# Attention outputs with queries on partitions, elementwise work off GpSimd, and a shorter reciprocal root

## The chip, the cores and the metric

One core of a Trainium2 chip runs the whole program. The metric is the device time of one execution in microseconds (us), as the median over runs. A profile shows one execution: its engines are TensorE (PE; PEld is its weight load), VectorE (DVE), ScalarE (ACT), GpSimd (POOL) and SyncE (SP, which issues the transfers).

## The reference

A first block (linear recurrence, long convolutions, 16 experts) is followed by two attention layers with MLPs, all in float32 on 512 positions of width 1024. The change lies in the attention layers and in the last norm. Each layer has four kinds of attention with four heads of 64 value columns: latent attention (M), differential attention (D), a window with sinks (S) and a neighbourhood with a bias table (N). Three of the four outputs get a norm over 256 columns, the differential one a norm per head:

```python
    for l in range(DEPTH_2):
        h = rms_norm(x, norm1_g[l])
        proj = h @ w_in[l]
        ...
        mix = jnp.concatenate([rms_norm(y_a, out_g_mla[l]), y_b,
                               rms_norm(y_c, out_g_swa[l]), rms_norm(y_d, out_g_na[l])], axis=-1)
        x = x + mix @ w_out[l]
        h = rms_norm(x, norm2_g[l])
        x = x + jnp.square(jax.nn.relu(h @ w_up[l])) @ w_down[l]
    return rms_norm(x, final_norm_g)
```

with, in every attention, `p = softmax(q k * scale)`, `o = p v`; in D `w = p0 - lam * p1`, `o = w v`, and `rms_norm(o, subln_g) * (1 - lambda_init)` for each head.

## The kernel before, in words

Activations lie with features on partitions and the 512 positions along the row, as 8 tiles `x` of 128 x 512. Large products are made of three passes on rounded halves (`mm3`, lines 161 to 165): each operand is split into a rounded part and the remainder (`split`, lines 147 to 158, the rounded part on ACT, the remainder on DVE or POOL). Weights stream through `WStream.get` (line 222) in the same manner.

A layer's attention (lines 398 to 842) is a list of steps written out by hand (`CFG["order0"]`, `CFG["order1"]`, lines 21 and 22; interpreted from line 792): projections (`b`, `c`, `d`, `v`, `u`), operands of the scores (`m`, `e`, `s`, `q`, `k`), pairs of heads in halves of two query blocks (`M0a`, `D1b`), norms (`nM`, `n0`, `n1`, `nS`, `nN`), the split of finished outputs (`x`) and the output projection in two parts (`W`, `V`). When the program is built, a planner places every instruction on its engine's queue by this order and by its own estimate of durations, and instructions then run in that order on each engine.

For one block of 128 queries and one head, `softmax_tile` (line 542) makes the scores in PSUM, DVE takes the row extreme, ACT the exponential with the row sum; M, S and N then scale the 128 x n tile by the reciprocal of the sum on DVE (`normed`, line 607). In D the second tile is folded into the first with a factor that holds both sums (lines 705 to 707), and the first sum is left to the norm. `transposed` (line 592) turns P by TensorE with up to four 128 x 128 transposes, and ACT (for M every other time DVE) copies it out. `pv` (line 610) then multiplies: V's 64 columns of a head are stationary, 128 queries stream, and the two heads of a pair write PSUM partitions 0 to 63 and 64 to 127 of one tile `o`, features on partitions:

```python
        for a, j in enumerate(js):
            for s in range(2):
                nc.tensor.matmul(o[s * 64:(s + 1) * 64, q], v[:, j, vc[s]:vc[s] + 64], pts[s][:, a],
                                 start=a == 0, stop=a == len(js) - 1)
```

`ysq` (line 631) copies `o` and squares it on ACT. `out_norm` (line 638) adds two squares on DVE, sums columns by matmuls with ones (line 190), takes the reciprocal root on DVE (`rsqrt`, lines 168 to 180, eleven small instructions), spreads the result over partitions by four diagonal tiles and a matmul (`bcast_cols`, line 204), and scales (line 647). `diff_norm` (line 711) does the same per head with two column sums (line 715) and two broadcasts into 64 partitions each (lines 726 to 730). `split_held` (line 627) splits the results on ACT and POOL.

On POOL in a layer are: the remainders of `hilo_rows` (line 539), of the S keys, the N keys (line 533), the small weights (line 493) and the outputs (line 625); and the two multiplies of `roped` (lines 449 and 450, for the b and c heads only the first). In the first layer also the remainders of the first three weight tiles (line 456). At the end of the program `last_half` (line 324) sums eight squares on DVE, and one of four final scalings is on POOL (line 347).

Of the kernel before, what the change touches and what calls it, by code (L numbers as in the profile page):

```python
# [6 lines left out]
F32 = mybir.dt.float32  # L7
F32R = mybir.dt.float32r
# [10 lines left out]
CFG = dict(acc=2, o=1, S=3, tp=2, qk=9, H=9, y=5, z=7, P=5, PT=2, sb=4, R=4, raw=3, sp=2, rp=3, rb=1,  # L19
           lm=1, le=0, ls=0, lq=0, lk=0, fM=2, fD=100, fS=100, fN=100, rB=1, rC=1, wi=1, wo=1, xs=0, ul=0,  # L20
# [147 lines left out]
def rsqrt(c, v, n):  # L168

    nc = c.nc  # L170
    t = c.small.tile([128, 8], I32, name="rq_t", tag="rq_t")[:, :n]
# [32 lines left out]
def bcast_cols(c, cols, psp, tag, out, scale=1.0):  # L204
# [8 lines left out]
    nc.scalar.activation(out, ps, AF.Copy, scale=scale)  # L213
    return ps
# [30 lines left out]
def body_t2(c, A, x, out, gain=None):  # L245
# [5 lines left out]
    with ExitStack() as ctx:  # L251
        ws = c.ws = WStream(c, ctx.enter_context(pool("w", 3, side="right")), CFG["raw"], CFG["sp"])
        pers = ctx.enter_context(pool("t2"))
        c.blk = pers.tile([128, 2], F32, name="blk")
        nc.vector.memset(c.blk, 0.0)
        nc.vector.memset(c.blk[0:64, 0:1], 1.0)
        nc.vector.memset(c.blk[64:128, 1:2], 1.0)
# [11 lines left out]
        def sumsq(tiles):  # L269
            s = None  # L270
            for t in tiles:
                q = hp.tile([128, T], F32, name="sq", tag="sq", bufs=3)
                nc.scalar.activation(q, t, AF.Square)
                if s is None:
                    s = q
                else:
                    nc.vector.tensor_tensor(s, s, q, op=OP.add)
            return s
# [45 lines left out]
        def last_half(l, ff, s, cols, mp):  # L324

            sq, xg = None, []
            for m in range(KD):
# [7 lines left out]
                if m == 0:  # L335
                    sq = q
                else:
                    nc.vector.tensor_tensor(sq, sq, q, op=OP.add)
# [4 lines left out]
            rb = mp.tile([128, T], F32, name="rbf", tag="rbf", bufs=2)[:, :256]  # L343
            ps = bcast_cols(c, rs, ps_t, "tp", rb)
# [53 lines left out]
def attention(c, A, l, h, rsb, cols, lam_init, ap, hp, ws, ps_acc, ps_o, ps_s, ps_t, x, rx, gain):  # L398
# [57 lines left out]
    e = "pool" if rx is not None else "dve"  # L456
    cq0 = compact(proj(0, acc=spsum, lo_eng=e, late=late), rsb)
    cq1 = compact(proj(1, 96, acc=spsum, lo_eng=e, late=late), rsb)
    ckv = compact(proj(2, acc=spsum, lo_eng=e, late=late), rsb)
    kpe = roped(cq1, 0, slice(64, 96))  # L460
# [44 lines left out]
    roped(qn[2], 0)  # L505
# [36 lines left out]
    def softmax_tile(passes, i, js, bias=None, op=OP.min, init=None, sm=None):  # L542
# [26 lines left out]
        if init is not None:  # L569
            es = c.small.tile([128, 1], F32, name="es", tag="es")  # L570
            nc.scalar.activation(es, init, AF.Exp, bias=mn, scale=sgn)
            nc.vector.tensor_tensor(sm, sm, es, op=OP.add)
# [34 lines left out]
    def normed(p, rc):  # L607
        nc.vector.tensor_scalar(p, p, rc, None, op0=OP.mult)
# [9 lines left out]
    def emit_mixed(z):  # L618
        held.append(z)

    def split_mixed(z):
        hi = hp.tile([128, T], F32R, name="hh", tag="hh")
        lo = hp.tile([128, T], F32R, name="hl", tag="hl")
        split(c, z, hi, lo, lo_eng=ENG[CFG["xs"]])
        mixed.append((hi, lo))
# [12 lines left out]
    def out_norm(yqs, g0, perm=False):  # L638
        (y0, q0), (y1, q1) = yqs
        nc.vector.tensor_tensor(q0, q0, q1, op=OP.add)  # L640
        r = rs_cols(c, q0, 256, ps_acc, "acc")
        rb = ap.tile([128, T], F32, name="rb", tag="rb", bufs=CFG["rb"])
        bcast_cols(c, r, ps_acc, "acc", rb)
        for i, y in enumerate((y0, y1)):
            z = ap.tile([128, T], F32, name="z", tag="z", bufs=CFG["z"])
            v = (lambda a: a.rearrange("p (w r) -> p w r", r=8)) if perm else (lambda a: a)
            nc.vector.scalar_tensor_tensor(wr(z) if perm else z, v(y), cols[:, g0 + i:g0 + i + 1], v(rb),
                                           op0=OP.mult, op1=OP.mult)
            emit_mixed(z)
# [18 lines left out]
    def mla_pair(pair, ops, o, tiles):  # L668
        for i in tiles:
            pts = []  # L670
            for s in range(2):
                p, sm = softmax_tile(ops[s], i, full)
                normed(p, reciprocal(sm))
                pts.append(transposed(p, full, "M"))
# [20 lines left out]
    def diff_pair(pair, ops, o, tiles):  # L695

        if pair not in sums:
            sums[pair] = ap.tile([128, 4, 2], F32, name="sms", tag="sms", bufs=2)
        sms = sums[pair]
# [11 lines left out]
    def diff_norm(yq, sms):  # L711
        y, q = yq
        ps = acc()
        for i in range(4):
            nc.tensor.matmul(ps[:, 2 * i:2 * i + 2], q[:, i * 128:(i + 1) * 128], c.blk, start=True, stop=True)
        v = c.small.tile([128, 8], F32, name="dv", tag="dv", bufs=2)
        u = c.small.tile([128, 8], F32, name="du", tag="du", bufs=2)
        rc = sms.rearrange("p i s -> p (i s)")
        nc.vector.reciprocal(rc, rc)
        nc.vector.tensor_tensor(u, rc, rc, op=OP.mult)  # L720
        nc.vector.tensor_tensor(v, u, ps[:, :8], op=OP.mult)
        nc.vector.tensor_scalar(v, v, 1.0 / 64, EPS, op0=OP.mult, op1=OP.add)
        r = rsqrt(c, v, 8)
        nc.vector.tensor_tensor(r, r, rc, op=OP.mult)
        rb = acc()
        for s in range(2):
            d = c.diag.tile([128, 4, 128], F32, name="diag", tag="diag")
            for i in range(4):
                nc.vector.tensor_scalar(d[:, i], c.ident, r[:, 2 * i + s:2 * i + s + 1], 1.0 - lam_init, op0=OP.mult, op1=OP.mult)
            nc.tensor.matmul(rb[s * 64:(s + 1) * 64], c.ones[:, :64], d.rearrange("p a b -> p (a b)"), start=True, stop=True)  # L730
        z = ap.tile([128, T], F32, name="z", tag="z", bufs=CFG["z"])
        nc.vector.scalar_tensor_tensor(z, y, cols[:, 25:26], rb, op0=OP.mult, op1=OP.mult)
        emit_mixed(z)
# [12 lines left out]

    def swa_pair(g, qs, o, tiles):
        for i in tiles:
# [3 lines left out]
            for n in range(2):  # L752
                p, sm = softmax_tile([(qs[n], kops[n][0]), (qs[n], kops[n][1])], i, js,
                                     bias=band[:, b0:b0 + 128 * len(js)], init=nsk[:, 2 * n + g:2 * n + g + 1])
                normed(p, reciprocal(sm))
                pts.append(transposed(p, js, "S"))
            pv(o, i, pts, vb, [256, 320], js)

# [9 lines left out]
    def na_pair(pair, ops, o, tiles):  # L768
        qs, ks = ops
        for i in tiles:  # L770
# [4 lines left out]
            for s in range(2):  # L775
                tab = ap.tile([128, 384], F32, name="nab", tag="sb", bufs=CFG["sb"])[:, :n]
                nc.sync.dma_start(tab, A["nab"][l, pair * 2 + s][:, at:at + n])
                p, sm = softmax_tile([(qs[s], ks[s][0]), (qs[s], ks[s][1])], i, js, bias=tab, op=OP.max)
                normed(p, reciprocal(sm))
# [12 lines left out]
    for step in CFG["order%d" % l].split():  # L792
# [35 lines left out]
        elif step in ("n0", "n1"):  # L828
            diff_norm(ys["D", n], sums[n])
        elif step == "nM":  # L830
            out_norm((ys["M", 0], ys["M", 1]), 19)
        elif step == "nS":
            out_norm((ys["S", 0], ys["S", 1]), 21)
        elif step == "nN":
            out_norm((ys["N", 0], ys["N", 1]), 23, perm=True)
# [982 lines left out]
```

## Time and profile before

| | |
|---|---|
| median of 3 runs | 2930.9 us (2928.51 to 2931.96) |
| the profiled execution's own time | 2928.38 us |
| its span in the profile | 2926.6 us |
| PE busy | 2782.9 us, 95% |
| DVE busy | 1541.2 us, 53% |
| ACT busy | 923.7 us, 32% |
| POOL busy | 177.5 us, 6% |

The busy share is a mean over stages with different limits. Attention of the first of the two layers lies at about 1575 to 1890 us of the span, of the second at 2253 to 2560, each followed by its MLP; the last MLP ends with the final norm and the stores. Matmuls are pipelined, so the busy time of a group of them holds their tails; the time that one costs is read from one start to the next.

### The profile page before, as it was taken

Reading aid. Unit: us, or ns where it says so; the run is one execution under the profiler, and the core shown is the slowest. Engines: PE = TensorE matmul, PEld = TensorE weight load, DVE = VectorE, ACT = ScalarE, POOL = GpSimd, SP = SyncE. Lnnn points to the kernel's source line nnn. Section 1 sums busy time; section 2 is a strip of 40 time slices with the busy share of each in tenths; the row PEclk is TensorE's granted clock in tenths of the full one; section 3 lists DMA queues with packets and bytes.
Section 4 is the critical chain, followed back from the end, with each engine's and each line's share of the span. In section 5 each row is a group of like instructions: output and inputs, shape, how many; then the busy total and the mean of one; then the engine's idle time right before and its main releaser. Section 6 shows DMA issues by size and latency. Waiting matters only on the chain.

```text
span 2926.6 us, 35016 instructions
## 1 busy us (share of the span) xinstructions
PE 2782.9 (95%) x13300; PEld 1844.3 (63%) x13300; DVE 1541.2 (53%) x3121; ACT 923.7 (32%) x1553; POOL 177.5 (6%) x150
## 2 busy tenths in 40 slices
PE   8999999999999999998898899999999999999998
PEld 6878888763333333333334676788887776788887
DVE  7878899642212212222114889654445789644436
ACT  5656332220000000000002367433323377433324
POOL 0000000000000000000000233000000333000000
PEclk9999999999999999999999999999999999999999
DMA  4443333589999999999996233223223332222223
GB/s 161 155 158 138 117 109 123 165 333 413 420 421 421 420 420 421 421 421 421 421 421 266 79 83 80 81 94 101 94 94 121 94 85 76 86 94 94 95 98 132
DMA packets 136352, 617.89 MB, mean 211 GB/s; under 512 B 17423, under 2 KB 31575, under 8 KB 84600
## 3 DMA queue, kind: packets, MB, share of 16 engines
q1 hardware_dynamic: 136184, 615.65, 55.6%
q8 instruction: 105, 1.72, 0.2%
q14 instruction: 63, 0.52, 0.1%
HBM read 582.03 MB, written 16.78 MB: 205 GB/s over the span
## 4 chain that ended last, share of the span: by engine, by line
PE 78%; DMA 8%; DVE 8%; issue 3%; ACT 1%; POOL 1%; SPq 0%; DVEq 0%; ACTq 0%; POOLq 0%
PE acc L165 11%; PE acc L164 11%; PE acc L163 11%; PE gps L1665 11%; DMA ew<-experts 8%; PE dps L1690 5%; PE S L163 4%; PE S L164 4%; PE S L165 4%; PE fps L1197 2%; PE o L615 2%; PE acc L1717 2%; PE acc L1618 2%; PE S L549 2%; PE tp L598 1%
## 5 line engine op out<-in xcount | busy, mean ns | idle before, releaser
L152 ACT CAST wh<-wr 128x1024 fp32r<-128x1024 f32 (+3 forms) x294 | 291.7, 993 | 819.5 <-PE acc L164 510.6
L1665 PE MATMUL gps<-ew,xe 128*64 128x512 f32 x2048 | 489.1, 597 | 9.1 <-DMA ew<-experts 8.9
L155 DVE TENSOR_TENSOR wl<-wr,wh 128x1024 fp32r<-128x1024 f32 (+3 forms) x291 | 335.8, 1156 | 68.7 <-ACT wh L152 67.8
L1665 PEld LDWEIGHTS gps<-ew,xe 128*64 128x64 f32 x2048 | 151.0, 137 | 286.0 <-issue 253.4
L163 PE MATMUL acc<-hh,wh 128*128 128x512 f32 x768 | 312.1, 406 | 0.1
L165 PE MATMUL acc<-hh,wl 128*128 128x512 f32 x768 | 307.2, 400 | 3.0 <-DVE wl L155 2.8
L164 PE MATMUL acc<-hl,wh 128*128 128x512 f32 x768 | 308.4, 402 | 0.0
L1690 PE MATMUL dps<-ew,hT 128*64 128x512 f32 x992 | 225.1, 600 | 15.2 <-DMA ew<-experts 8.8
L164 PE MATMUL acc<-fl,wh 128*128 128x512 f32 (+1 forms) x576 | 213.5, 371 | 0.0
L165 PE MATMUL acc<-fh,wl 128*128 128x512 f32 (+1 forms) x576 | 213.4, 371 | 0.0
L163 PE MATMUL acc<-fh,wh 128*128 128x512 f32 (+1 forms) x576 | 213.2, 370 | 0.0
L165 PE MATMUL S<-hh,wl 128*128 128x512 f32 x512 | 199.9, 391 | 0.0
L164 PE MATMUL S<-hl,wh 128*128 128x512 f32 x512 | 199.0, 389 | 0.0
L163 PE MATMUL S<-hh,wh 128*128 128x512 f32 x512 | 198.9, 389 | 0.0
L1673 DVE TENSOR_TENSOR g<-g,gps 128x512 f32<-128x512 f32 x32 | 21.9, 685 | 331.0 <-PE gps L1665 322.3
L1690 PEld LDWEIGHTS dps<-ew,hT 128*64 128x64 f32 x992 | 74.8, 138 | 156.4 <-issue 128.4
L165 PEld LDWEIGHTS acc<-hh,wl 128*128 128x128 f32 x768 | 145.8, 190 | 37.3 <-DVE wl L155 6.3
L163 PEld LDWEIGHTS acc<-hh,wh 128*128 128x128 f32 x768 | 146.3, 191 | 35.7 <-issue 6.1
L164 PEld LDWEIGHTS acc<-hl,wh 128*128 128x128 f32 x768 | 146.1, 190 | 31.8 <-issue 4.2
L395 DVE TENSOR_TENSOR x<-acc,x 128x512 f32<-128x512 f32 x56 | 38.8, 692 | 184.2 <-PE acc L165 184.2
L1672 ACT ACTIVATE g<-gps 128x512 f32<-128x512 f32 x32 | 19.2, 599 | 366.3 <-PE gps L1665 353.8
L379 DVE SCALAR_TENSOR_TENSOR r<-S,rsb 128x512 f32<-128x512 f32 x64 | 44.1, 692 | 162.3 <-PE S L165 158.6
(400 smaller groups left out, 4503.5 us busy)
## 6 DMA issues: line engine op xcount, KB each, us to landing
ew<-experts SPq DMA_DIRECT2D x384, 1024.0 KB, 19.8
wr<-w_down SPq DMA_DIRECT2D x72, 512.0 KB, 3.3
wr<-w_up SPq DMA_DIRECT2D x64, 512.0 KB, 3.3
wr<-w_in SPq DMA_DIRECT2D x56, 512.0 KB, 4.5
wr<-in_w SPq DMA_DIRECT2D x38, 512.0 KB, 3.3
R<-qkc SPq DMA_DIRECT2D x72, 128.0 KB, 2.3
filters_dram<-K SPq DMA_DIRECT2D x8, 1024.0 KB, 3.9
K<-filters_dram SPq DMA_DIRECT2D x8, 1024.0 KB, 6.7
```

Of the source, the lines that this page charges most:

```text
L152: nc.scalar.copy(hi, src)
L155: (nc.vector if lo_eng == "dve" else nc.gpsimd).tensor_tensor(lo, src, hi.bitcast(F32), op=OP.subtract)
L163: nc.tensor.matmul(ps, W[0], X[0], start=start, stop=False)
L164: nc.tensor.matmul(ps, W[0], X[1], start=False, stop=False)
L165: nc.tensor.matmul(ps, W[1], X[0], start=False, stop=stop)
L549: nc.tensor.matmul(ps, q[:, qs], k[:, ks], start=a == 0, stop=a == len(passes) - 1)
L615: nc.tensor.matmul(o[s * 64:(s + 1) * 64, q], v[:, j, vc[s]:vc[s] + 64], pts[s][:, a], start=a == 0, stop=a == len(js) - 1)
L1197: nc.tensor.matmul(ps[:, half * Q:(half + 1) * Q], dft[:, s], v[:, r], start=True, stop=True)
L1618: nc.tensor.matmul(ps[h * 64:(h + 1) * 64], sel[:, i], rows[i][h], start=i == 0, stop=i == 3)
L1665: nc.tensor.matmul(ps[h * 64:(h + 1) * 64], xes[e][:, kt], W[:, k, h * T:(h + 1) * T], start=kt == 0, stop=kt == 7)
L1690: nc.tensor.matmul(outs[e][col * 64:(col + 1) * 64], hT[:, j, p * 64:(p + 1) * 64], W[:, p, h * T:(h + 1) * T], start=cc == 0 and j == 0 a ...
L1717: nc.tensor.matmul(ps, Y[f // 4][j][:, (f % 4) * 128:(f % 4 + 1) * 128], st[f // 4], start=j == 0, stop=j == n - 1)
```

## The change

1. `pv` swaps its operands: P is stationary (128 x 128), a head's 64 V columns stream, and the output has queries on partitions, with the two heads side by side along the row. All key blocks of the first head come before those of the second.
2. M, S and N no longer scale P. The row sums of a pair go into a small tile (128 x 4 blocks x 2 heads), as in D before. `ysq` adds a row sum of the squares per block and head on DVE. The norms work on these small tiles: reciprocals, squares, a sum over heads for M, S and N, `rsqrt`, and one multiply of the 128 x 512 output by the factors (`scaled_rows`). Column sums, diagonals and broadcasts of the output norms are gone.
3. `split_held` first transposes each finished output (four 128 x 128 transposes into PSUM), and the split applies the gain, the rounded part on ACT and the remainder on DVE.
4. All remainders and the multiplies of `roped` go to DVE; so does the last scaling at the end, straight from PSUM.
5. `rsqrt` has nine instructions instead of eleven.
6. `sumsq` and `last_half` hand the last square to the column-sum matmuls as a second tile instead of adding it on DVE.

```diff
-           lm=1, le=0, ls=0, lq=0, lk=0, ..., rB=1, rC=1, wi=1, wo=1, xs=0, ul=0,
+           lm=1, le=1, ls=1, lq=1, lk=1, ..., rB=2, rC=2, wi=1, wo=1, ul=1,
...
 def rsqrt(c, v, n):
-    nc.vector.tensor_scalar(t, v.bitcast(I32), 1, None, op0=OP.logical_shift_right)
-    nc.vector.tensor_scalar(y.bitcast(I32), t, -1.0, 1597463007.0, op0=OP.mult, op1=OP.add)
-    for _ in range(3):
-        nc.vector.tensor_tensor(u, y, y, op=OP.mult)
-        nc.vector.scalar_tensor_tensor(u, u, -0.5, v, op0=OP.mult, op1=OP.mult)
-        nc.vector.scalar_tensor_tensor(y, u, 1.5, y, op0=OP.add, op1=OP.mult)
+    nc.vector.tensor_scalar(y.bitcast(I32), v.bitcast(I32), -0.5, 1597463007.0, op0=OP.mult, op1=OP.add)
...
+    nc.vector.tensor_scalar(w, u, 1.5, 2.5, op0=OP.mult, op1=OP.add)
+    nc.vector.tensor_tensor(w, w, u, op=OP.mult)
+    nc.vector.scalar_tensor_tensor(y, w, 1.875, y, op0=OP.add, op1=OP.mult)
...
-                if j == 0:
-                    nc.gpsimd.tensor_tensor(t, t, rb[:, None, :].to_broadcast([128, 2, 256]), op=OP.mult)
-                else:
-                    nc.vector.tensor_tensor(t, t, ps[:, None, :].to_broadcast([128, 2, 256]), op=OP.mult)
+                nc.vector.tensor_tensor(t, t, ps[:, None, :].to_broadcast([128, 2, 256]), op=OP.mult)
...
     def pv(o, i, pts, v, vc, js):
-        q = slice(i * 128, (i + 1) * 128)
-        for a, j in enumerate(js):
-            for s in range(2):
-                nc.tensor.matmul(o[s * 64:(s + 1) * 64, q], v[:, j, vc[s]:vc[s] + 64], pts[s][:, a],
+        for s in range(2):
+            for a, j in enumerate(js):
+                nc.tensor.matmul(o[:, i * 128 + s * 64:i * 128 + (s + 1) * 64], pts[s][:, a], v[:, j, vc[s]:vc[s] + 64],
                                  start=a == 0, stop=a == len(js) - 1)
...
     def split_held():
         while held:
-            split_mixed(held.pop(0))
+            y, g, perm = held.pop(0)
+            ps = ps_t.tile([128, T], F32, name="tp", tag="tp")
+            for i in range(4):
+                nc.tensor.transpose(ps[:, i * 128:(i + 1) * 128], y[:, i * 128:(i + 1) * 128], c.ident)
...
+                split(c, ps, hi, lo, scale=g)
...
     def ysq(o):
         nc.scalar.copy(y, o)
-        nc.scalar.activation(q, y, AF.Square)
-        return y, q
+        nc.scalar.activation(q, o, AF.Square)
+        ss = ap.tile([128, 4, 2], F32, name="ss", tag="ss", bufs=4)
+        nc.vector.tensor_reduce(ss, q.rearrange("p (i s n) -> p i s n", i=4, s=2), axis=AX.X, op=OP.add)
+        return y, ss
+
+    def scaled_rows(y, f, g, perm=False):
+        v = y.rearrange("p (i s n) -> p i s n", i=4, s=2)
+        nc.vector.tensor_tensor(v, v, f[:, :, :, None].to_broadcast([128, 4, 2, 64]), op=OP.mult)
+        held.append((y, g, perm))
```

## Rows read from the trace of the kernel before

**Rows 1.** The page's busy times of TensorE.
```profile
PE 2782.9 (95%) x13300; PEld 1844.3 (63%) x13300; DVE 1541.2 (53%) x3121; ACT 923.7 (32%) x1553; POOL 177.5 (6%) x150
```
**Rows 2.** Stretches: us, then PE, PEld, DVE, ACT, POOL busy, clock, DMA share, GB/s.
```profile
1575.00:1890.00 315.00, 291.77 (x1573) 213.55 (x1573) 254.38 (x620) 169.72 (x376) 83.61 (x56) 0.96 0.28 81
2253.00:2560.00 307.00, 291.82 (x1586) 218.20 (x1585) 239.94 (x592) 168.34 (x372) 78.73 (x53) 0.98 0.31 91
2372.00:2432.00 60.00, 57.10 (x331) 41.78 (x329) 57.60 (x98) 45.91 (x104) 26.93 (x18) 1.00 0.33 90
2432.00:2475.00 43.00, 39.58 (x252) 27.15 (x251) 37.44 (x165) 29.32 (x86) 8.98 (x7) 0.96 0.32 83
```
**Rows 3.** TensorE's waits, 2253 to 2560: us in total, times, longest.
```profile
PE bc_ps L212 <- DVE diag L210: 3.6, 1, 3.6
PE tp L598 <- DVE rc L577: 2.4, 2, 1.5
PE acc L730 <- DVE diag L729: 2.4, 1, 2.4
```
**Rows 4.** Groups of instructions, 2253 to 2560: busy us, mean ns, idle before.
```profile
L615 PE MATMUL o<-PT,vb 128*64 128x128 f32 x208 | 21.8, 284 | 0.8 <-ACT PT L602 0.8
L615 PE MATMUL o<-PT,va 128*64 128x128 f32 x128 | 12.2, 282 | 0.1
L615 PE MATMUL o<-PT,vd 128*64 128x128 f32 x80 | 9.5, 288 | 0.2 <-ACT PT L602 0.2
...
L730 PE MATMUL acc<-diag,ones 128*64 128x512 f32 x8 | 4.7, 672 | 2.4 <-DVE diag L729 2.4
```
**Rows 5.** TensorE's timeline around a long run: start us, us, line.
```profile
2368.90 0.40 PE L163 MATMUL acc<-hh,wh 128*128 128x512 f32 x1
2369.23 1.09 PE L615 MATMUL o<-PT,va 128*64 128x128 f32 x14
...
2370.82 0.39 PE L163 MATMUL acc<-hh,wh 128*128 128x512 f32 x1
```
**Rows 6.** The same around a short run.
```profile
2397.68 0.39 PE L163 MATMUL acc<-hh,wh 128*128 128x512 f32 x1
2398.00 0.43 PE L615 MATMUL o<-PT,vb 128*64 128x128 f32 x2
...
2398.93 0.40 PE L549 MATMUL S<-H 96*128 96x512 f32 x1
```
**Rows 7.** The same around column sums with one streamed column.
```profile
2563.99 0.39 PE L164 MATMUL S<-hl,wh 128*128 128x512 f32 x1
2564.21 0.98 PE L190 MATMUL rs_ps<-ones,sq 128*128 128x1 f32 x8
...
2565.37 0.40 PE L163 MATMUL S<-hh,wh 128*128 128x512 f32 x1
```
**Rows 8.** VectorE's timeline: first and eleventh instruction of a root.
```profile
2529.01 0.16 DVE L174 TENSOR_SCALAR rq_t<-rs_v 128x4 int32<-128x4 int32 x1
...
2530.98 0.16 DVE L179 SCALAR_TENSOR_TENSOR rq_y<-rq_u,rq_y 128x4 f32<-128x4 f32 x1
```
**Rows 9.** VectorE's groups, 2253 to 2560.
```profile
L707 DVE SCALAR_TENSOR_TENSOR P<-P,rc 128x512 f32<-128x512 f32 x16 | 15.1, 946 | 0.0
L450 DVE TENSOR_TENSOR rp_b<-rp_b,rope 128x512 f32<-128x512 f32 x7 | 11.3, 1616 | 0.0
...
L608 DVE TENSOR_SCALAR P<-P,rc 128x512 f32<-128x512 f32 x16 | 8.0, 503 | 0.1
...
L155 DVE TENSOR_TENSOR H<-R,H 96x512 fp32r<-96x512 f32 x8 | 5.4, 682 | 2.3 <-ACT H L152 1.6 <-PE S L549 0.6
```
**Rows 10.** GpSimd's largest group, 2253 to 2560.
```profile
L539 POOL TENSOR_TENSOR H<-R,H 32x512 fp32r<-32x512 f32 (+1 forms) x24 | 34.2, 1426 | 80.0 <-ACT H L538 77.3 <-issue 2.0
```
**Rows 11.** The end of the program: VectorE's last add, SP's last stores.
```profile
2914.05 0.42 DVE L338 TENSOR_TENSOR sq<-sq 128x256 f32<-128x256 f32 x1 [0.54 <-ACT sq L334]
...
2921.20 1.97 SPq L350 DMA_DIRECT2D out_dram<-xg  x4
```

More of the change, by code (lines that the diff above doesn't have):

```diff
@@ L201, in rs_cols, with bcast_cols @@
     return rsqrt(c, v, n)
-def bcast_cols(c, cols, psp, tag, out, scale=1.0):
+def bcast_cols(c, cols, psp, tag, out=None, scale=1.0):
     nc = c.nc
@@ L212, in bcast_cols @@
     nc.tensor.matmul(ps, c.ones, d.rearrange("p a b -> p (a b)")[:, :n * 128], start=True, stop=True)
-    nc.scalar.activation(out, ps, AF.Copy, scale=scale)
+    if out is not None:
+        nc.scalar.activation(out, ps, AF.Copy, scale=scale)
     return ps
@@ L270, in sumsq @@
             s = None
-            for t in tiles:
+            for k, t in enumerate(tiles):
                 q = hp.tile([128, T], F32, name="sq", tag="sq", bufs=3)
@@ L275, in sumsq @@
                     s = q
+                elif k == len(tiles) - 1:
+                    s = [s, q]
                 else:
@@ L455, in attention @@
     late = True
[L456 to L460, printed above, removed]
+    cq0 = compact(proj(0, acc=spsum, late=late), rsb)
+    cq1 = compact(proj(1, 96, acc=spsum, late=late), rsb)
+    ckv = compact(proj(2, acc=spsum, late=late), rsb)
+    kpe = roped(cq1, 0, slice(64, 96), dve=2)
     def lsq(a):
@@ L634, in ysq, with out_norm @@
         q = hp.tile([128, T], F32, name="sq", tag="sq", bufs=3)
-        nc.scalar.activation(q, y, AF.Square)
-        return y, q
[L638 to L649, printed above, removed]
+        nc.scalar.activation(q, o, AF.Square)
[6 more added lines that the diff above has]
+        held.append((y, g, perm))
+    def out_norm(mix, g0, perm=False):
+        f = sums[mix]
+        nc.vector.reciprocal(f, f)
+        u = ap.tile([128, 4, 2, 2], F32, name="fu", tag="fu", bufs=2)
+        nc.vector.tensor_tensor(u, f, f, op=OP.mult)
+        for p in range(2):
+            nc.vector.tensor_tensor(u[:, :, p], u[:, :, p], ys[mix, p][1], op=OP.mult)
+        v = c.small.tile([128, 4], F32, name="rs_v", tag="rs_v")
+        nc.vector.tensor_reduce(v, u.rearrange("p i a s -> p i (a s)"), axis=AX.X, op=OP.add)
+        nc.vector.tensor_scalar(v, v, 1.0 / 256, EPS, op0=OP.mult, op1=OP.add)
+        r = rsqrt(c, v, 4)
+        f = f.rearrange("p i a s -> p i (a s)")
+        nc.vector.tensor_tensor(f, f, r[:, :, None].to_broadcast([128, 4, 4]), op=OP.mult)
+        for p in range(2):
+            scaled_rows(ys[mix, p][0], sums[mix][:, :, p], cols[:, g0 + p:g0 + p + 1], perm)
     full = [0, 1, 2, 3]
@@ L668, in mla_pair @@
     def mla_pair(pair, ops, o, tiles):
+        sms = pair_sums("M", pair)
         for i in tiles:
@@ L671, in mla_pair @@
             for s in range(2):
-                p, sm = softmax_tile(ops[s], i, full)
-                normed(p, reciprocal(sm))
+                p, sm = softmax_tile(ops[s], i, full, sm=sms[:, i, s:s + 1])
                 pts.append(transposed(p, full, "M"))
@@ L695, in diff_pair @@
     def diff_pair(pair, ops, o, tiles):
-        if pair not in sums:
-            sums[pair] = ap.tile([128, 4, 2], F32, name="sms", tag="sms", bufs=2)
-        sms = sums[pair]
+        sms = pair_sums("D", pair)
         for i in tiles:
@@ L709, in diff_pair, with diff_norm @@
             pv(o, i, pts, vb, [pair * 128, pair * 128 + 64], full)
[L711 to L715, printed above, removed]
+    gd = ap.tile([128, 1], F32, name="gd")
+    nc.vector.tensor_scalar(gd, cols[:, 25:26], 1.0 - lam_init, None, op0=OP.mult)
+    def diff_norm(pair):
+        y, ss = ys["D", pair]
+        rc = sums["D"][:, :, pair]
         v = c.small.tile([128, 8], F32, name="dv", tag="dv", bufs=2)
         u = c.small.tile([128, 8], F32, name="du", tag="du", bufs=2)
-        rc = sms.rearrange("p i s -> p (i s)")
+        w = lambda a: a.rearrange("p (i s) -> p i s", i=4)
         nc.vector.reciprocal(rc, rc)
-        nc.vector.tensor_tensor(u, rc, rc, op=OP.mult)
-        nc.vector.tensor_tensor(v, u, ps[:, :8], op=OP.mult)
+        nc.vector.tensor_tensor(w(u), rc, rc, op=OP.mult)
+        nc.vector.tensor_tensor(w(v), w(u), ss, op=OP.mult)
         nc.vector.tensor_scalar(v, v, 1.0 / 64, EPS, op0=OP.mult, op1=OP.add)
         r = rsqrt(c, v, 8)
[L724 to L733, printed above, removed]
+        nc.vector.tensor_tensor(rc, rc, w(r), op=OP.mult)
+        scaled_rows(y, rc, gd)
     sk = ap.tile([128, 4], F32, name="sk")
@@ L745, in swa_ops @@
         return [hilo_rows(stack([(cqt[g][n * 64:(n + 1) * 64], d) for d in (0, 64)]), 128, slice(64, 128), "s") for n in range(2)]
+    sinks = {}
     def swa_pair(g, qs, o, tiles):
+        sms = pair_sums("S", g)
+        if g not in sinks:
+            sinks[g] = ap.tile([128, 4, 2], F32, name="snk", tag="snk", bufs=2)
         for i in tiles:
@@ L753, in swa_pair @@
                 p, sm = softmax_tile([(qs[n], kops[n][0]), (qs[n], kops[n][1])], i, js,
-                                     bias=band[:, b0:b0 + 128 * len(js)], init=nsk[:, 2 * n + g:2 * n + g + 1])
-                normed(p, reciprocal(sm))
+                                     bias=band[:, b0:b0 + 128 * len(js)], init=nsk[:, 2 * n + g:2 * n + g + 1],
+                                     sm=sms[:, i, n:n + 1], es=sinks[g][:, i, n:n + 1])
                 pts.append(transposed(p, js, "S"))
             pv(o, i, pts, vb, [256, 320], js)
+        if tiles[-1] == 3:
+            nc.vector.tensor_tensor(sms, sms, sinks[g], op=OP.add)
     def na_ops(pair):
@@ L769, in na_pair @@
         qs, ks = ops
+        sms = pair_sums("N", pair)
         for i in tiles:
@@ L828, in attention @@
         elif step in ("n0", "n1"):
[L829 removed]
+            diff_norm(n)
         elif step == "nM":
[L831 removed]
+            out_norm("M", 19)
         elif step == "nS":
[L833 removed]
+            out_norm("S", 21)
         elif step == "nN":
[L835 removed]
+            out_norm("N", 23, perm=True)
         elif a == "x":
```

48 lines of the change are left out of this document (24 added, 24 removed).

## The prediction, made before the change was run

> **What bounds the kernel now.** I read the page's busy times first: TensorE works 95% of the span [rows 1], so time is gained only by giving it less to do or by taking away its waits. The change touches the two attention layers and the last microseconds; the rest (the first block, the experts, the MLPs) keeps its instructions. The table of stretches shows both layers [rows 2]: 315 and 307 us long, TensorE busy 291.8 in each, so 15 and 23 us of plain waiting. VectorE is busy 240 to 254 us, and in the middle of layer 1 it is the fuller engine: 57.6 of 60 us in the stretch in which the differential heads run, beside TensorE's 57.1. GpSimd has 79 to 84 us a layer there. The list of TensorE's waits [rows 3] names the largest: 3.6 us for the diagonal tiles of the last output norm (nN), 2.4 for those of the differential norm (n1), 2.4 in two places where a softmax reciprocal is late. Busy time flatters a pipelined engine, so I priced matmuls from start to start in the timeline: a 512-column product takes 0.23 us.
>
> **The change part by part.** Both layers run the same code and show the same counts, so I cost layer 1 and double it.
>
> *P times V.* A layer has 416 records of this product (208 matmuls of two records each) [rows 4]. Now a head's 64 V columns are the stationary operand and 128 queries stream; two heads sit in the two column halves and run side by side. Fourteen such records between two products take from 2368.90 to 2370.82, and with the three 512-column slots (0.69) taken off, 1.23 us [rows 5]. At 0.055 us a record (128 columns side by side; seven pairs in 0.76) some 0.4 us of that is no work: the products on either side are spread out. A pair alone costs 2398.93 - 2397.68 - 0.69 = 0.56 us, of which 0.11 would be work [rows 6]. Each query block of a pair of heads makes one such short and one longer run, since the first head's P is ready earlier: 64 runs in the layer. So now 416 x 0.055 + 64 x 0.42 = 49.8 us. After, a 128 x 128 P is stationary and 64 V columns stream over the whole array, no two heads at once. No row has this shape; the nearest are the norm's matmuls with a full stationary tile and one column: eight records cost 2565.37 - 2563.99 - 0.46 = 0.92 us, 0.115 each, the boundaries in it [rows 7]. 416 x 0.115 = 47.8 us: 2.0 less. From below, 0.105 (their own start to start, 0.84 for eight) gives -6; from above, if the 64 columns came on top of the load as half of a 128-column slot of 0.11, 0.17 a record, +21. I take 0.115: full tiles with one column and full 128-column transposes run at nearly the same rate, so columns hide behind the load.
> The Trainium skill, TensorE: Matmul & The Clock Gate, section "Back-to-back issue gap", gives about 81 ns for a load and a matmul of 128 columns in a stream. By it this term would be 416 x 0.081 = 33.7, 14 us less in a layer; the rows here say 115, and the sum goes by them.
>
> *Norms on TensorE.* Gone in a layer: eight records of column sums in each of three output norms and two differential ones, 5 x 0.92 = 4.6, and the broadcasts of the norm factors: three of two records of 512 columns, and eight records of 64 x 512, which are busy 4.7 us, 0.59 each with their tails [rows 4]; between that and the 0.23 of a product in one pass I take 0.43: 14 x 0.43 = 6.0. Added: 32 transposes at 0.11, 3.5, and eight more column-sum records (a sum of squares goes to the matmul as two tiles), 0.9. Net -6.2.
>
> *Waits.* The 2.4 us at n1 goes with its broadcast; the clock in that stretch fell to a mean of 0.96 [rows 2], about 1.2 us more. At nN TensorE no longer stands in the middle of the chain: off it come a 0.68 add, 0.92 of sums, two of eleven root instructions at 0.2 (the first starts at 2529.01, the eleventh at 2530.98) [rows 8], 0.88 of diagonals; on it a row sum (0.68), four small operations (0.8), one scaling (0.69). I let the 3.6 us wait shrink to 1.5, with 0.7 for the clock: -2.8. Together -6.4.
>
> *VectorE and GpSimd.* All elementwise work of GpSimd in these layers goes to VectorE. Two-operand work on 512 columns takes VectorE 0.68 us [rows 9] and GpSimd 1.43 [rows 10], and GpSimd also stretches VectorE: a multiply of the rotation, both operands in SBUF, lasts 1.62 us beside it, the differential combine 0.95 [rows 9]. Over the layer VectorE loses 48 normalisations of P (0.50 at 512 columns [rows 9], 24 us), their 48 reciprocals, 28 diagonals, 8 final scalings and the stretch (7 multiplies and 16 combines, 10 us), and gains 53 moved operations, 8 row sums and 8 scalings, 69 x 0.68 = 47 us: about even, beside 240 of 307 us busy [rows 2]. But the differential heads lose no normalisation: in that stretch 18 GpSimd operations (26.9 us, [rows 2]) become 18 x 0.68 = 12.2 on VectorE, and only some 8 of stretch goes (16 combines at 0.2, as many small products, a few others). 57.6 + 4.2 is 61.8 us of work in 60: its reciprocals come a little later, and TensorE waits there. I charge 3 us a layer. The queue of SP gains by this: its copies into stacked tiles wait for rotated heads that are done sooner. GpSimd has nothing behind the moved work.
>
> *Other edits.* Root shortened by two small instructions, the final add before the column sums dropped, the last scaling off GpSimd: hidden everywhere but at the end. There the 0.42 us add [rows 11] and two root steps (0.4) go, and the first of four output stores, which kept the others queued on SP, no longer waits for a GpSimd multiply of twice VectorE's duration [rows 9, 10], 0.7: -1.5 us in all.
>
> Sum: a layer -2.0 - 6.2 - 6.4 + 3 = -11.6; two layers -23.2, with the end -24.7. The profiled execution took 2928.4 us (span 2926.6 and 1.8 around it), 2.5 under the median 2930.9 of the runs; the difference taken from the median gives **2906 us**.
>
> **The rivals.**
> *Slower: the spread at the edges of a run is not the column halves' and stays.* Then the product costs 416 x 0.112 + 64 x 0.42 = 73.5, 23.7 more than now; with the other terms (-9.6) a layer is 14.1 slower, with the end 26.7 in all: 2958. It decides once fewer than half of the 27 us at the edges go away. For it: two heads side by side do stream at half the price, and that is certainly lost. Against: the one-column records follow and precede the same products with almost no spread [rows 7]. The same comes out if the columns add to the load (0.17).
> The Trainium skill, TensorEngine Tiling (Array Packing), section "When to Use Tiling", speaks against the change: where the streamed side has 64 columns it advises to swap the operands and use two column halves, which is the form being left. The rows agree on streaming (0.055 against 0.115), not on the cost of going in and out.
> *VectorE becomes the bound.* The differential stretch ends 3 us later still, and the eight transposed outputs, each holding one of two PSUM tiles for a copy and a subtract, hold up the softmax transposes 3 us: 5.6 a layer, 12.7 with the end: 2918. For it: 57.6 of 60. Against: VectorE has room on either side, and the build may place moved work there.
> *Nothing to measure.* The waits that go come back elsewhere and P times V gains nothing: -6.2 + 6 a layer, 2929.
> *All of it.* The product at 0.105, no charge in the differential stretch, nN's wait gone: -6 - 6.2 - 10 a layer, 2885.
> That the change does not do what it says I can leave out: every GpSimd operation of these layers has its counterpart on VectorE in the diff.
>
> **How the numbers follow.** What a measurement here can tell from no change is about 0.2%, 6 us. Forecast (2893 to 2913): 0.50. VectorE bound: 0.20. All of it: 0.09. Nothing: 0.09. Slower: 0.12. The range reaches from the 2885 of the case that gets all of it to the 2929 of the null case, and leaves out the slower case and the upper half of the null one. Faster by over 0.2%: 0.79; within: 0.09; slower: 0.12.
>
> **What would show it.** After: the product's records 416 a layer at 0.11 from start to start, and neighbours at their usual 0.23; no waits for diagonals of n1 and nN, but transposes waiting there at most 2 us; no GpSimd work in the layers; the multiplies of the rotation at 0.68; VectorE near full beside the differential heads. Wrong would be: 0.17 or more a record, spread that stays at the edges, or a wait of several microseconds in front of the transposed outputs.

## The result, and the profile after

| | before | after |
|---|---|---|
| median of 4 runs | 2930.6 us (2928.51 to 2931.96) | 2910.8 us (2906.83 to 2911.88) |
| span of the profiled execution | 2926.6 us | 2908.5 us |

The ratio is 0.9935, 95% interval 0.9923 to 0.9947: faster by 0.65%, and inside the forecast of 2893 to 2913. The page's busy times of the kernel after, which answer to [rows 1]:

```profile
PE 2777.9 (96%) x13288; PEld 1885.1 (65%) x13288; DVE 1501.8 (52%) x2952; ACT 919.0 (32%) x1545; POOL 12.6 (0%) x39
```

The time was not gained where the prediction put it. Here are the same instructions' starts in both timelines, as changes of each stretch (us):

| stretch | layer 1 | layer 0 |
|---|---|---|
| second latent projection to the first score | -8.2 | -9.2 |
| M: first score to its last P times V | 0.0 | 0.0 |
| D and S: to their last P times V | **+11.4** | **+10.6** |
| N: from there to its last P times V | -6.7 | -6.7 |
| to the first down product of the MLP | -6.1 | -6.1 |
| MLP, and the way to the next layer or the last product | +1.4 | +2.5 |

With 0.8 us lost before the layers and 1.7 gained after the last MLP product the sum is the 18.1 us by which the span shrank. So the output norms paid off; beside that, the projections ahead of the first score gave 8 to 9 us a layer that no term of the sum held, and the differential heads took back 11.

The table of stretches shows both. For the kernel after: all of layer 1's attention, its projections, M, the differential stretch, and the worst 28 us in it (columns as in [rows 2]):

```profile
2245.00:2542.00 297.00, 287.29 (x1565) 236.31 (x1564) 221.95 (x512) 164.71 (x368) 0.00 (x0) 0.97 0.31 91
2245.00:2318.00 73.00, 73.00 (x338) 58.80 (x337) 55.47 (x120) 23.36 (x37) 0.00 (x0) 1.00 0.37 117
2318.00:2355.00 37.00, 37.00 (x262) 32.53 (x260) 24.91 (x39) 23.66 (x55) 0.00 (x0) 1.00 0.20 51
2355.00:2424.00 69.00, 63.23 (x315) 51.17 (x313) 57.63 (x119) 45.86 (x104) 0.00 (x0) 0.85 0.28 73
2375.00:2403.00 28.00, 24.34 (x100) 19.47 (x98) 21.18 (x42) 18.30 (x45) 0.00 (x0) 0.63 0.31 78
```

*Projections.* The kernel before needed 82 us for them, and its TensorE waited twice there; the stretch and its waits:

```profile
2253.00:2335.00 82.00, 78.29 (x341) 62.27 (x340) 59.09 (x116) 25.48 (x38) 22.38 (x13) 0.96 0.36 114
```
```profile
PE rs_ps L190 <- DVE lsq L469: 2.0, 1, 2.0
PE S L163 <- ACT va L516: 1.7, 1, 1.7
```

Those 3.7 us of waiting and 4% of clock (3.3 us) are gone: TensorE is now busy for all of 73 us at a granted clock of 1.00.

*Differential heads.* [Rows 2] had 60 us with 57.10 busy at 1.00; now it is 69 us. VectorE's busy time is the same 57.6 us, so it is not the fuller engine. TensorE's idle time went from 2.9 to 5.8 us, and a mean clock of 0.85 over 69 us is 10.4 us lost. TensorE's waits of the layer, which answer to [rows 3]:

```profile
PE o L615 <- ACT PT L600: 4.2, 6, 1.0
PE S L549 <- ACT P L568: 1.5, 2, 1.4
PE tp L674 <- DVE qkc L441: 1.5, 2, 0.9
PE tp L624 <- DVE y L646: 0.7, 1, 0.7
PE acc L163 <- ACT hh L157: 0.6, 1, 0.6
PE acc L164 <- DVE hl L158: 0.4, 1, 0.4
PE tp L596 <- DVE rc L575: 0.3, 1, 0.3
```

The waits for diagonals are gone, and the transposed outputs of nN wait 0.7 us, its products another 1.0. New are the waits for ACT among the differential heads. TensorE's timeline where they begin:

```profile
2379.16 0.48 PE L164 MATMUL acc<-hl,wh 128*128 128x512 f32 x1
2381.00 0.50 PE L549 MATMUL S<-H 96*128 96x512 f32 x1 [1.36 <-ACT P L568]
2381.66 0.49 PE L549 MATMUL S<-H 96*128 96x512 f32 x1 [0.16 <-ACT P L568]
2382.49 1.09 PE L596 MATMUL tp<-ident,P 128*128 128x128 f32 x4 [0.34 <-DVE rc L575]
2384.31 1.97 PE L615 MATMUL o<-vb,PT 128*128 128x64 f32 x8 [0.73 <-ACT PT L600]
...
2388.40 1.97 PE L615 MATMUL o<-vb,PT 128*128 128x64 f32 x8 [0.30 <-ACT PT L600]
...
2392.49 1.97 PE L615 MATMUL o<-vb,PT 128*128 128x64 f32 x8 [0.73 <-ACT PT L600]
```

and VectorE's, with four remainders in a row ahead of a combine that TensorE needs:

```profile
2378.74 2.82 DVE L539 TENSOR_TENSOR H<-R,H 32x512 fp32r<-32x512 f32 x4 [0.26 <-ACT H L538]
2381.60 0.75 DVE L720 SCALAR_TENSOR_TENSOR P<-P,rc 128x512 f32<-128x512 f32 x1
2382.26 0.15 DVE L575 RECIPROCAL rc<-sm 128x1 f32<-128x1 f32 x1
```

From 2379 to 2397 TensorE's queue holds nothing but the heads themselves, in the end one in 4.1 us (2384.31, 2388.40, 2392.49). The granted clock is 1.00 until 2382 and 0.50 from 2384 to 2402, the lower of its two levels, 1.2 GHz; eight P times V records that show 1.00 us at 2373.05 show 1.97 there. In the kernel before, other products stood between the heads all through the first pair.

### The profile page after: what moved, and what is told of

It reads as the page before. It is cut to its first block, busy times and chain, and to the rows that moved or that the text cites. A ratio compares the mean times of both kernels' runs of the same rounds, so it can differ in the third digit from the quotient of the medians.

```text
span 2908.5 us, 34625 instructions
## 1 busy us (share of the span) xinstructions
PE 2777.9 (96%) x13288; PEld 1885.1 (65%) x13288; DVE 1501.8 (52%) x2952; ACT 919.0 (32%) x1545; POOL 12.6 (0%) x39
## 4 chain that ended last, share of the span: by engine, by line
PE 80%; DMA 10%; DVE 5%; issue 2%; ACT 2%; POOL 0%; SPq 0%; DVEq 0%; ACTq 0%; POOLq 0%
PE acc L165 11%; PE acc L164 11%; PE acc L163 11%; PE gps L1678 10%; DMA ew<-experts 10%; PE dps L1703 5%; PE S L165 4%; PE S L163 4%; PE S L164 4%; PE o L615 3%; PE fps L1210 2%; PE S L549 2%; PE tp L596 2%; PE acc L1730 2%; PE acc L1631 2%
```

## The experiments

Each line of results gives the median, and the ratio to the kernel before with its interval.

**Which part gives the time back?**

One group back on GpSimd:
```diff
-           lm=1, le=1, ls=1, ...
+           lm=1, le=0, ls=1, ...
```


> The changed kernel with the remainders of the differential operands (16 a layer) back on GpSimd, all else as changed. Theory 1 (these remainders stand on VectorE between the differential heads, TensorE waits, falls to its lower clock for some 20 us and loses about 10 us a layer): granted clock 1.00 in that stretch again, 8 to 10 us a layer back, 2911 - 18 = 2893 us (2887 to 2901). Theory 2 (the prediction's: VectorE is late by 3 us a layer, and GpSimd would stretch its neighbours again): 2905 to 2911. Theory 3 (the stretch is longer because of the swapped P times V and its copies of P): no change, 2911, and the clock still falls.

2908.3 us, 0.9927 (0.9913 to 0.9942). Theory 1 missed by 15 us. The fall of the clock in the first pair did go (clock 1.00 from 2380 to 2410), but a wait of 3.7 us for the value projection's scaling came in front of the heads, and the clock fell in another place, to 0.73 and 0.59 in the two slices from 2410, where VectorE makes the remainders of the S operands.

All of it back:
```diff
-           lm=1, le=1, ls=1, lq=1, lk=1, ..., rB=2, rC=2, ..., ul=1,
+           lm=1, le=0, ls=0, lq=0, lk=0, ..., rB=1, rC=1, ..., ul=0,
...
-    cq0 = compact(proj(0, acc=spsum, late=late), rsb)
+    cq0 = compact(proj(0, acc=spsum, lo_eng=e, late=late), rsb)
...
-    kpe = roped(cq1, 0, slice(64, 96), dve=2)
+    kpe = roped(cq1, 0, slice(64, 96))
...
-    roped(qn[2], 0, dve=2)
+    roped(qn[2], 0)
```


> The changed kernel with every moved elementwise operation of the layers back on GpSimd (remainders of the operands and of the small weights, first multiplies of the rotation, remainders of the first three weight tiles of the first layer); the swapped P times V, the norms on small tiles, the root and the end stay as changed. Theory 1 (remainders among the differential heads cost 10 us a layer, rotations off GpSimd gain 8 us a layer before the first scores): 2911 - 20 + 16 = 2907 us (2900 to 2914), with the waits of 2.0 and 1.7 us before the first scores back. Theory 2 (prediction: moving cost 3 us a layer and gained nothing): 2905. Theory 3 (the loss is the swapped P times V's, the move gained 8 us a layer): 2927.

2912.0 us, 0.9942 (0.9927 to 0.9957): taken together, the move of all that work was worth next to nothing. Both waits before the first scores are back (2.0 and 1.7), but now 4.9 us are lost between M and D. VectorE's queue shows by what (columns: start, us):

```profile
2366.53 0.68 DVE L441 TENSOR_TENSOR qkc<-acc,rsb 128x512 f32<-128x512 f32 x1
2367.13 0.92 DVE L181 TENSOR_SCALAR rq_w<-rq_u 128x4 f32<-128x4 f32 x1
...
2371.43 1.21 DVE L182 TENSOR_TENSOR rq_w<-rq_w,rq_u 128x4 f32<-128x4 f32 x1
2372.57 0.68 DVE L452 TENSOR_TENSOR qkc<-qkc,rp_b 128x512 f32<-128x512 f32 x1
2373.17 1.22 DVE L183 SCALAR_TENSOR_TENSOR rq_y<-rq_w,rq_y 128x4 f32<-128x4 f32 x1
2374.43 0.17 DVE L663 TENSOR_TENSOR sms<-sms,rq_y 128x16 f32<-128x16 f32 x1
2374.63 1.29 DVE L647 TENSOR_TENSOR y<-y,sms 128x512 f32<-128x512 f32 x2
2375.84 0.68 DVE L441 TENSOR_TENSOR qkc<-acc,rsb 128x512 f32<-128x512 f32 x1
```

M's new output norm stands in front of the second `qkc`, for which TensorE waits, and while GpSimd works small steps of 128 x 4 take 0.92 to 1.22 us instead of 0.16. GpSimd at that time, and TensorE's wait:

```profile
2366.72 1.29 POOL L540 TENSOR_TENSOR H<-R,H 32x512 fp32r<-32x512 f32 x1 [1.74 <-DMA R<-qkc]
...
2371.04 3.33 POOL L540 TENSOR_TENSOR H<-R,H 32x512 fp32r<-32x512 f32 x2
```
```profile
PE tp L675 <- DVE qkc L441: 4.9, 1, 4.9
```

The Trainium skill, GPSIMD Engine Reference, section "8. Key points", says that GpSimd shares its SBUF interfaces with VectorE and contends with VectorE instructions that have two SBUF inputs or run in a two-port mode. The trace agrees on two inputs (`rq_w<-rq_w,rq_u`, 1.21 us), and shows that an operation of 512 elements in all pays as much as a large one.

The move alone, on the kernel before (`le=1, ls=1, lq=1, lk=1, rB=2, rC=2, xs=1, ul=1`, the two `roped` calls with `dve=2`, `e = "dve"`):

> The kernel before with only the engines changed: every elementwise operation of the layers from GpSimd to VectorE, as in the change, with the remainders of the outputs; P times V, norms, root, column sums and the end stay as before. Theory 1: about even, 2930.6 - 16 + 20 = 2935 us (2928 to 2941), the clock falls to 0.50 among the differential heads. Theory 2: 2930.6 + 6 = 2937, without a fall of the clock. Theory 3: 2930.6 - 16 = 2915.

2940.0 us, 1.0034 (1.0022 to 1.0047), slower. Its timeline gains 8.6 and 7.2 us before the first scores of the two layers and loses 14.8 and 14.2 in D and S, with the clock down to 0.52 in layer 0 and to 0.67 in layer 1.

**Its two halves, each alone on the kernel before**

```diff
-rB=1, rC=1,
+rB=2, rC=1,
...
-    kpe = roped(cq1, 0, slice(64, 96))
+    kpe = roped(cq1, 0, slice(64, 96), dve=2)
...
-    roped(qn[2], 0)
+    roped(qn[2], 0, dve=2)
```


> The kernel before with only the multiplies of the rotation of the b heads, of the latent key part and of the latent queries taken from GpSimd to VectorE (7 tiles a layer); all else as before. Theory D (the 8 us a layer that the change gains ahead of the first scores are these multiplies', on GpSimd and beside it, with the waits of 2.0 and 1.7 us and the clock that falls after them): 2930 - 2 x 6 to 2 x 8 = 2916 us (2913 to 2920). Rival (the gain there comes from the norms' small tiles, the remainders of the small weights or the shorter root): 2927 to 2931.

2917.7 us, 0.9965 (0.9953 to 0.9977). These are eight multiplies on six tiles (the expectation miscounts them). Ahead of the first score 7 us are gained in layer 1 (-4.3 us against the kernel before at the second latent projection, -11.2 at the first score), but only some 3 in layer 0 (-2.1 at that projection, -5.4 at M's last P times V). In layer 1 that stretch has no wait left:

```profile
2248.00:2325.00 77.00, 76.96 (x351) 61.15 (x350) 59.52 (x126) 25.74 (x39) 6.80 (x5) 1.00 0.39 124
```

```diff
-           lm=1, le=0, ls=0,
+           lm=1, le=1, ls=0,
```


> The kernel before with only the remainders of the differential operands (16 a layer) on VectorE instead of GpSimd; all else as before. Theory A/B (these remainders among the differential heads make TensorE wait for VectorE, and its clock falls): 2930 + 2 x 8 to 2 x 11 = 2948 us (2940 to 2954), with the granted clock at 0.5 to 0.7 for some 20 us of each differential stretch. Rival (the prediction's: about 3 us a layer, less what GpSimd no longer stretches): 2930 to 2937, clock at 1.00.

2950.5 us, 1.0076 (1.0061 to 1.0091). So eight multiplies and sixteen remainders, moved from GpSimd to VectorE at 0.68 us each, are worth 5 us a layer one way and 10 the other. But the clock did not have to fall for that: in layer 1 it did, to 0.74 in one slice of 10 us, and in layer 0 it stayed at 1.00, for a loss nearly as large. D and S in layer 0, from the last P times V of M to that of S, in three kernels: before, this one, and the changed one:

```profile
1713.80:1810.60 96.80, 92.85 (x579) 68.11 (x577) 90.15 (x240) 74.40 (x186) 33.57 (x24) 1.00 0.34 89
```
```profile
1716.10:1822.70 106.60, 94.66 (x574) 67.59 (x571) 91.50 (x258) 74.33 (x186) 18.68 (x13) 1.00 0.32 83
```
```profile
1705.40:1812.80 107.40, 101.53 (x564) 84.68 (x563) 84.69 (x213) 71.54 (x181) 0.00 (x0) 0.90 0.29 77
```

Both lose 10 us: here as idle time of TensorE (11.9 us instead of 4.0) at a clock of 1.00, in the changed kernel mostly as clock (10.7 us). VectorE has 1.4 us more work than before here, and 5.5 less in the changed kernel. What the two have in common is the order: heads stand alone, without cover (512-column products that depend on no head and can run while a head waits), and there TensorE waits; products stand together elsewhere, and there VectorE is idle (in this kernel busy 9.6 of 10 us from 1740 to 1760, and 5.3 in the next 10).

**Order or remainders?**

```diff
-... D0a e1 D0b D1a u1 k c1 s0 D1b ...
+... D0a e1 u1 D0b D1a k c1 s0 D1b ...
```


> The changed kernel with one step of the order moved: the values of N's second block (u1, 24 products of 512 columns and their transposes) ahead of the second half of the first differential pair (D0b) instead of behind the first half of the second (D1a); engines, work and remainders as in the change. Theory A (in the differential stretch VectorE sets the pace; heads with no other product between them leave TensorE waiting, and its clock falls): the first pair has cover, the fall of the clock there goes, four heads of the second pair lose theirs; 2911 - 2 x 5 = 2901 us (2893 to 2908). Theory B (the four remainders in a row on VectorE are the cause, whatever stands between the heads): the burst still stands there, 2908 to 2914.

2910.7 us, 0.9942 (0.9927 to 0.9957). Theory A's number was wrong. The fall left the first pair and came in the second, whose cover had been taken away, and D and S lose 11.0 us in layer 1, about as much as before the move (11.4). Slices of layer 1:

```profile
2380.00:2390.00 10.00, 10.00 (x62) 8.49 (x61) 9.19 (x17) 8.20 (x19) 0.00 (x0) 1.00 0.43 119
...
2400.00:2410.00 10.00, 8.21 (x33) 5.93 (x33) 8.63 (x20) 5.73 (x15) 0.00 (x0) 0.67 0.00 0
2410.00:2420.00 10.00, 8.18 (x29) 6.19 (x28) 6.42 (x13) 5.66 (x14) 0.00 (x0) 0.50 0.24 54
2420.00:2430.00 10.00, 9.74 (x46) 8.70 (x47) 9.11 (x27) 4.19 (x10) 0.00 (x0) 0.64 0.13 42
```

The fall moved with the cover.

```diff
-H=9, ... m1 M1a M1b c2 v0 e0 D0a e1 D0b ...
+H=13, ... m1 M1a e0 M1b c2 v0 D0a e1 D0b ...
```


> The changed kernel with 13 instead of 9 operand tiles and the operands of the first differential pair (e0) ahead of M's last half, so that their eight remainders and most of the second pair's run on VectorE before the heads. Theory B (remainders between the heads): the burst of four is gone, 2911 - 2 x 5 = 2901 us (2894 to 2906). Theory A (cover): nine heads of the first pair and a half stand with no other product between them, so TensorE still waits on VectorE's pace of about 2.3 us a head and the clock falls: 2908 to 2918.

2906.5 us, 0.9929 (0.9909 to 0.9949), between the two. D and S lose 6.9 us instead of 11.4 in layer 1, and 4.5 instead of 10.6 in layer 0; in layer 1 a fall to 0.58 for some 10 us is left. The remainders' place has a share, but not all.

Holding M's norm back, on the kernel with all work on GpSimd (instructions of the block are queued behind the last differential combine on their engine, without a wait):
```diff
-                nc.vector.scalar_tensor_tensor(p1, p2, rc2, p1, op0=OP.mult, op1=OP.add)
+                c.hold = nc.vector.scalar_tensor_tensor(p1, p2, rc2, p1, op0=OP.mult, op1=OP.add)
...
-            out_norm("M", 19)
+            with tc.issue_after(c.hold.ins):
+                out_norm("M", 19)
```


> The kernel with all moved work back on GpSimd, and M's output norm (its small operations and two scalings on VectorE) held back on VectorE's queue until the last differential combine; nothing else. Theory C (M's norm, stretched by GpSimd to 1.2 us for some of its small operations, stands on VectorE in front of the value projection's scaling, and TensorE waits 4.9 us and loses 2 to 3 us of clock there, in each layer): 2912 - 2 x 6 = 2900 us (2895 to 2905). Rival (the wait is that of the rotation and the weight remainder beside GpSimd, which stand there too): 2909 or more.

2899.1 us, 0.9907 (0.9892 to 0.9922), as theory C had it: 13 us in both layers together for the place of one norm. The same hold on the changed kernel, with `le=0, ls=0, lk=0`:

> The changed kernel with the remainders of the D and S operands and the S keys on GpSimd (rotations, N keys, small weights and first weight tiles stay on VectorE), and M's output norm held back until the last differential combine. If A to C are right together, no fall of the clock is left in the differential stretch of either layer: the second hole of the kernel with only D's remainders on GpSimd (0.59 to 0.73 of the clock for 15 us) goes as well, 2908 - 2 x 8 = 2892 us (2886 to 2899). Rival (VectorE's work in that stretch sets its length however it is ordered): 2904 or more.

2903.8 us, 0.9920 (0.9905 to 0.9934), at the rival's end. A fall to 0.69 from 2410 to 2420 is left; the rotations of the c heads are still on VectorE there.

These go back too, with the remainders of the N operands; rotations before the first scores, small weights and first weight tiles stay on VectorE (`le=0, ls=0, lq=0, lk=0, rB=2, rC=1, ul=1`, and the hold):

> The changed kernel with the remainders of the D, S and N operands and the c rotations on GpSimd as before, the other rotations, the small weights and the first weight tiles on VectorE as in the change, and M's output norm held back until the last differential combine. Theories A, C and D together (gain of about 8 us a layer ahead of the first scores kept, nothing given back in the differential stretch): 2899 - 2 x 6 = 2887 us (2881 to 2893). Rival (what the rotations gain is given back in the differential stretch in any case): 2897 or more.

**2889.8 us, 0.9867 (0.9850 to 0.9883)**: the best of all, twice the gain of the change. Its layer 1 and its differential stretch:

```profile
2227.00:2515.00 288.00, 279.90 (x1573) 230.33 (x1572) 212.87 (x478) 164.11 (x366) 47.54 (x33) 1.00 0.33 96
2355.00:2415.00 60.00, 56.89 (x345) 47.74 (x344) 57.92 (x127) 45.37 (x104) 21.66 (x16) 1.00 0.41 107
```

The clock is at 1.00 throughout both, and the 60 us of the kernel before are back, with the same 57 to 58 us of work on both engines.

```diff
+    e = "pool" if rx is not None else "dve"
-    cq0 = compact(proj(0, acc=spsum, late=late), rsb)
+    cq0 = compact(proj(0, acc=spsum, lo_eng=e, late=late), rsb)
```
(and so for the other two)

> The same, with the remainders of the first three weight tiles of the first layer on GpSimd as before. If the 5.8 us for which the first products of the first layer wait for ScalarE's rounded weights cost time of their own: 3 to 5 us less than the kernel mixed. If they only take the place of the waits that GpSimd's remainders bring (2.4 us and others there): within 2 us of it.

2891.1 us, 0.9873 (0.9858 to 0.9887): within 2 us of `mixed`, so the 5.8 us wait at the first layer's entry only takes the place of the waits that GpSimd's remainders bring.

The last one, on `mixed`, takes the cover away and leaves no remainders of D on VectorE:
```diff
-... D1a u1 k c1 s0 D1b d1 d0 ...
+... D1a D1b u1 k c1 s0 d1 d0 ...
...
+        if step == "u1":
+            held_by = c.last_pv
+        if step in ("u1", "c1", "d1", "d0"):
+            with tc.issue_after(held_by.ins):
...
```


> The kernel mixed with the projections c1, d1, d0 and the values u1 (96 products of 512 columns a layer, 22 us of TensorE) held back on TensorE's queue until the last P times V of the differential heads; remainders of the operands on GpSimd, so none on VectorE between the heads. By VectorE's pace alone (two row extremes, two small ones, one combine: about 2.3 us a head, 16 heads, then the 22 us) a layer is some 5 us longer: 2890 + 2 x 5 = 2900 us (2893 to 2908) if the clock stays at 1.00 (theory B: only the remainders between the heads make it fall). Theory A (without other products TensorE, which needs 1.8 us a head, waits on VectorE, its clock falls, and the heads then take about 4 us each as in the changed kernel): 15 to 25 us a layer longer, 2920 to 2940, with the granted clock near 0.5 over most of the 16 heads.

2950.7 us, 1.0073 (1.0057 to 1.0090): 30 us a layer over `mixed`, more than even theory A had. The start of the heads, and the 50 us after:

```profile
2380.00:2390.00 10.00, 6.94 (x28) 4.57 (x26) 8.81 (x16) 5.79 (x13) 5.65 (x4) 0.92 0.36 87
2390.00:2440.00 50.00, 44.77 (x166) 35.65 (x164) 29.33 (x64) 30.32 (x74) 12.21 (x10) 0.50 0.19 53
```

VectorE is busy 29 of those 50 us, so it no longer sets the pace; TensorE itself does, at half its clock, and it did not come out of it while the heads ran alone. So missing cover is enough by itself, without a remainder on VectorE between the heads. That the remainders do their harm by changing where the planner puts the cover, and by delaying the heads that then stand alone, fits `rem_only`, `values_earlier` and `d_operands_early`, but is argued: no run keeps the order of the kernel before and moves the remainders alone.

## Why the prediction was right, and where it was not

**The total was right by some luck: a gain of 8 to 9 us a layer that the sum did not hold and a loss that it had 8 us too small nearly cancel.**

*Rotations, not priced.* The prediction quoted the multiplies at 1.62 us beside GpSimd, counted them in VectorE's sum, and said of their effect only that SP's queue gains. They lie on the path to the first score. Of the 8.2 us gained there in layer 1 the run with the rotations alone shows 7; of the 9.2 in layer 0 it shows some 3, and what gives the rest there is not settled.

*"I charge 3 us a layer" in the differential stretch* came to 11. The step set VectorE's total against the length of the stretch, 61.8 us in 60. The total was 57.6, and `mixed` and the kernel before carry as much in 60 us. What the step missed is that with both engines at 57 of 60 us bunching costs: moving the 16 remainders changes where the independent products stand (`rem_only` against the kernel before), and the heads without them ran at VectorE's pace or, once the clock had fallen, at TensorE's lower one. Idle time did grow by about the 3 us charged (5.8 against 2.9); the 10.4 us of clock came on top. How much of that the clock costs by itself in the changed kernel is not settled, since the run with the remainders alone pays the same in waits.

*P times V, forecast -2.0 a layer, came to some 1 to 2 more than before.* The groups after, which answer to [rows 4], and a run of one head:

```profile
L615 PE MATMUL o<-vb,PT 128*128 128x64 f32 x208 | 31.3, 296 | 4.3 <-ACT PT L600 4.2
L615 PE MATMUL o<-va,PT 128*128 128x64 f32 x128 | 16.4, 271 | 0.0
L615 PE MATMUL o<-vd,PT 128*128 128x64 f32 x80 | 11.7, 278 | 0.0
```
```profile
2372.73 0.48 PE L549 MATMUL S<-H 96*128 96x512 f32 x1
2373.05 1.00 PE L615 MATMUL o<-vb,PT 128*128 128x64 f32 x8
2373.86 0.48 PE L164 MATMUL acc<-hl,wh 128*128 128x512 f32 x1
2374.18 0.39 PE L549 MATMUL S<-H 96*128 96x512 f32 x1
```

Records follow each other at 0.11, as forecast; but the run takes 2374.18 - 2372.73 - 2 x 0.23 = 0.99 us, 0.124 a record, since the products on either side still stand apart (0.32 instead of 0.23). By that a layer costs 416 x 0.124 = 51.6 against the 49.8 worked out for before. M, full on TensorE in both kernels, agrees in sign: its first score to its last P times V takes 35.7 us in both, with 61 products of 512 columns in it before and 59 after, so its 256 records cost two products, 0.46 us, more. The slower rival's spread thus stays in part, some 0.1 us a run, not 0.42. No run has the swapped P times V alone, so these are readings of the traces.
The Trainium skill, TensorE: Matmul & The Clock Gate, section "Back-to-back issue gap", gives about 81 ns for a load and a matmul of 128 columns in a stream; the records here, with 64 columns, stand at 112 ns, so the sum by the row was the better one.

*Norms and waits, -6.2 and -6.4.* Between the first score and the MLP's down product `mixed`, with the moves in that stretch undone but for the remainders of the outputs, shows -10.6 in layer 0 and -12.4 in layer 1, beside -14.6 forecast with P times V; with P times V 1 to 2 us dearer instead of 2 cheaper, norms and waits came out about as forecast. n1's wait is gone; nN keeps 1.7 us where 1.5 was forecast. By [rows 2] the clock around n1 is 4% of 43 us, 1.7 instead of the 1.2 charged. Behind that stretch stand the additional column sums, where 1.4 us are lost in layer 1 and 2.5 in layer 0, charged 0.9: the prediction counted eight more records a layer, and the trace has sixteen, as two norms a layer hand over a second tile.

*VectorE and GpSimd by the piece.* Groups of VectorE after:

```profile
L539 DVE TENSOR_TENSOR H<-R,H 32x512 fp32r<-32x512 f32 (+1 forms) x24 | 16.3, 684 | 3.8 <-ACT H L538 3.2
L720 DVE SCALAR_TENSOR_TENSOR P<-P,rc 128x512 f32<-128x512 f32 x16 | 11.9, 743 | 0.1
...
L450 DVE TENSOR_TENSOR qkc<-qkc,rope 128x512 f32<-128x512 f32 (+1 forms) x9 | 6.2, 686 | 0.1
```

All as forecast: 0.68 for a remainder, 946 down to 743 ns for the combine, 0.69 for a multiply of the rotation.

*End of the program.* 1.5 us forecast, 1.7 found.

*Rivals.* "VectorE becomes the bound" has the right place and the wrong mechanism. "All of it", 2885, was not reached by the change. `mixed`, in which no charge is left in the differential stretch, came within 5 us of it, but with the gain ahead of the first score, which that rival did not hold.

## What to carry to other kernels

Where two engines are both nearly full in a stretch, look at how their work is interleaved and not at its sums: independent products spread among chains that depend on another engine are worth more than their own time (22 us of products held back cost 30 a layer, through waits and the clock that follows them). A move between engines is a sum over places: the same 0.68 us operation gained where it ended a wait and lost where it stood in front of one, so move by stage and not by kind. Where a planner places instructions, look in the new trace for what it moved forward into a busy queue, as with M's norm, before judging the change itself.

## What the runs showed of the hardware

TensorE's clock fell to the 1.2 GHz level with no wait above 1.36 us ahead of it in the changed kernel's layer 1 and none above 1.45 in that of `no_cover`; in `no_cover` it stayed there for 50 us with TensorE busy 44.8 of 50, and in the changed kernel it was back at 1.00 by 2404, after a run of 512-column products from 2398. The Trainium skill, TensorE: Matmul & The Clock Gate, section "HAM oscillation — how this bites in real kernels", tells of a kernel whose waits between bursts bring the clock down each time; the trace agrees on the kind of cause, with far shorter waits and a fuller engine. Not settled is why `d_operands_early`, with seven heads in a row without cover (2378 to 2395 in layer 1), lost a quarter or less of what `no_cover` did.
